# Last column of a mixture-of-experts tail: the last pair's combine ahead of the gate products, one gather pass and one gain row moved, overflow counts made earlier

## The chip, the core and the metric

The kernel runs on one core of a Trainium2 chip. The metric is the device time of one execution in microseconds (us). The core has five engines with an instruction queue each: TensorE (PE, matrix products), VectorE (DVE), ScalarE (ACT), GpSimd (POOL) and SyncE (SP, which here issues the DMA transfers of weights and output rows). Each engine works through its own queue in order and waits on semaphores of the others.

## The reference

One decoder layer on 512 tokens of width 1024: a mixer (windowed attention and an mLSTM), cross-attention into 256 memory tokens, and a mixture of 64 experts; each of the three is followed by a layer norm of `alpha*h + branch`. The change lies in the third part:

```
g_sel = argmax(h @ w_router_group + b)                 # 1 of 8 groups
top_val, top_idx = top_k(expert logits of that group, 2)
weights = p_group * softmax(top_val)                   # 2 experts for a token
for each expert e, for its tokens x:
    y = (silu(x @ w_gate[e]) * (x @ w_up[e])) @ w_down[e]
moe[token] += weight * y
out = layer_norm(alpha*h + moe, ln3_g, ln3_b)
```

w_gate and w_up are 1024x256 and w_down 256x1024 for each expert, float32: three times 1 MB, 192 MB for the 64 experts.

## The kernel before

**Columns.** The expert part starts at about 720 us of the profile. The 1024 assignments of tokens to experts are put into 21 columns of 128 slots; a column serves 4 experts with 32 slots, 2 with 64, or 1 with 128. Two columns make a pair, whose tokens are gathered together by products with one-hot matrices (`gather`, L1261 and L1262, px copied to XT by ACT and DVE in `to_XT`, L1184 and L1182). For a column, `hidden` makes 8 x 4 gate products and as many up products for four experts (L1204, 64 instructions each in the profile), Silu on ACT (L1209) and the multiply with the up products on DVE (L1210); then come two transposes, a copy, the down products (L1285), a split of the scaled result into a high and a low part (`split`, L255 on ACT, L256 on DVE), and for each pair `combine`: one-hot products in eight tiles of 512 columns through two PSUM buffers (L1430), each added into the stream h by DVE (L1431). An assignment that finds no slot goes to an overflow loop behind the columns; its expert list and count (`ovi`) are made on DVE and moved by one PE transpose (`poe`) while columns 0 to 2 run.

**Weights.** Ten slots of 1 MB in SBUF are a ring that SP fills in order of use (L167, L171). A load into a slot waits for the last product that read it. The down weights of the last column (L184) are loaded in 12 pieces: for four experts columns 0 to 511, then 512 to 767, then 768 to 1023.

**The last column (c = 20).** It is alone, and its rows are finished without a combine. Its gate products (u = 0 in `hidden`) are followed by a hook at (0, 7), `rows_meanwhile`, in PE's order ahead of the up products. The hook holds the combine of the last pair (columns 18 and 19, tiles `pc_last`), then three gather passes `slot_rows` (L1578), which bring the stream's rows of the last column's tokens into PSUM tiles `zf` (512, 256 and 256 columns, 4 products each). Beside them the final layer norm runs for four row tiles of 128 tokens, each 128x1024: `stats` (bn_stats, L1531), `rsqrt2` for two row tiles (`ve` on DVE, L1537, and a power on POOL, L97), `shift2` (`nb`, DVE, L1542), `norm_row` (ACT, L1564), `gain_row` (DVE, L1567), `bias_row` (L1570; rows 0 and 1 on POOL, rows 2 and 3 on DVE) and a store by SP (L1571). The out tiles of these rows lie in two slots of the weight ring. Behind the up products come Silu, multiply, transposes `ph_l` (L1621), the copy (L1623), the down products `pd_l` (L1631), split, the products that add them to `zf` (L1635), bn_stats (L1637), the last norm steps on DVE and an indirect store from POOL (L1645) that writes the rows of the last column's tokens.

**Order.** For DVE and ACT the order of this part is that of the code (a manual schedule is switched on at L1525); PE and SP follow the order of the code, too. PSUM tiles come from pools, and a tile waits for the readers of the tile that had its bank before.

Of the kernel before, what the change touches and what calls it, by code (L numbers as in the profile page):

```python
# [10 lines left out]
F32 = mybir.dt.float32  # L11
# [5 lines left out]
ALU = mybir.AluOpType  # L17
AX = mybir.AxisListType
PSUM = bass.MemoryType.PSUM

P = 128
# [10 lines left out]
NE = 64  # L32
# [29 lines left out]
def tile_layer(ctx, tc, x, mem, positions, w_in, attn_sinks, conv_w, conv_b, b_igate, b_fgate, ml_norm_g,  # L62
# [4 lines left out]
    V, A, G, T = nc.vector, nc.scalar, nc.gpsimd, nc.tensor  # L67
# [11 lines left out]
    def tap(name, ap):  # L79
        if taps is not None and name in taps:  # L80
            nc.sync.dma_start(taps[name], ap)
# [13 lines left out]
    def rsqrt_cols(dst, src, n):  # L95

        G.tensor_tensor(dst, src, pow_h.to_broadcast([P, n]) if n > 1 else pow_h, ALU.pow)  # L97

    class LayerNorm:
# [7 lines left out]
        def stats(self, c):  # L107
            V.bn_stats(self.st[:, c, :], self.r[:, c * 512:(c + 1) * 512])
# [107 lines left out]
    work = scope.enter_context(tc.tile_pool(name="work_a", bufs=2))  # L216
# [32 lines left out]
    def split(hi, lo, src, scale=None, on=V):  # L249

        if scale is None:
            A.copy(hi, src)
            on.tensor_tensor(lo, src, hi.bitcast(F32), ALU.subtract)
        else:
            A.activation(hi, src, AF.Copy, scale=scale)  # L255
            V.scalar_tensor_tensor(lo, src, scale, hi.bitcast(F32), op0=ALU.mult, op1=ALU.subtract)  # L256
# [57 lines left out]
    def run(gen):  # L314
        for _ in gen:
            pass
# [432 lines left out]
    work = scope.enter_context(tc.tile_pool(name="work_x", bufs=2, reuse_waits="tile"))  # L749
# [81 lines left out]
    work = scope.enter_context(tc.tile_pool(name="work_y", bufs=2, reuse_waits="tile"))  # L831
# [80 lines left out]
    work = Arena(poolY, "arenaR")  # L912
    scr_at = 0
    R = work.tile([P, 8, P], name="R")
    iota_f = keep.tile([P, S], F32, name="iota_f")
    G.iota(iota_f, pattern=[[1, S]], base=0, channel_multiplier=0, allow_small_or_imprecise_dtypes=True)
    iota_p = work.tile([P, 1], name="iota_p")
# [37 lines left out]
    scr64 = work.tile([P, 1, NE], F32, name="scr64")  # L955
# [299 lines left out]
    def gather(g, XT, tag, pool, n=256):  # L1255

        for c in range(4):
            px = pool[0].tile([P, 2, 256], F32, name=f"px{tag}{c}", tag=pool[1])
            for j in range(2):
                for t in range(NT):  # L1260
                    T.matmul(px[:, j, :n], lhsT=h2hv[:, t, 2 * c + j, :], rhs=g[:, t, :n], start=(t == 0), stop=False)  # L1261
                    T.matmul(px[:, j, :n], lhsT=h2lv[:, t, 2 * c + j, :], rhs=g[:, t, :n], start=False, stop=(t == NT - 1))  # L1262
            to_XT(XT, px, c, n)
            yield
# [24 lines left out]
    def pair_onehots(tag):  # L1289
        t = strm.tile([P, 1056], F32R, name=f"oh{tag}", tag="wr", bufs=4)  # L1290
        return [t[:, i * S:(i + 1) * S] for i in range(2)]

    def scaled(pds, tok, wcol, oh, tag):

        yh = strm.tile([P, 1056], F32R, name=f"yh{tag}", tag="wh", bufs=2)[:, :D]
        yl = strm.tile([P, 1056], F32R, name=f"yl{tag}", tag="wl", bufs=2)[:, :D]
        V.tensor_scalar(oh, iota_f, tok, None, op0=ALU.is_equal)
        for nh, pd in enumerate(pds):
            ns = slice(nh * 512, (nh + 1) * 512)
            split(yh[:, ns], yl[:, ns], pd, wcol)  # L1300
        return yh, yl, oh

    exc = key
    ovend = work.tile([P, NE], F32, name="ovend")
    ovst = work.tile([P, NE], F32, name="ovst")
# [47 lines left out]
    pds01 = [[next(down0)]]  # L1353
# [5 lines left out]
    pds01.append(list(down(first[1], parts_of(1), "1", (psA, "psA"))))  # L1359
    used[0] += COLS[0][0] + COLS[1][0]  # L1360
    wstream.ahead(used[0] + len(wslots))
    gi = work.tile([P, 2, NT * 2], I32, name="gi")
    cs_ = work.tile([P, 2, NT * 2], F32, name="cs_")
    gflat = gslot.rearrange("p t k -> p (t k)")
# [21 lines left out]
    wtab = keep.tile([P, NCOL], F32, name="wtab")  # L1386
    tokf = keep.tile([P, NCOL], F32, name="tokf")
    g1 = gather(G1, XTs[1], "1", (psB, "psB"))
# [2 lines left out]
        T.matmul(ptab[:, :2 * NCOL], lhsT=R[:, i, :], rhs=CV[:, i].rearrange("p a c -> p (a c)"), start=(i == 0), stop=(i == 7))  # L1391
    V.tensor_scalar(wtab, ptab[:, 0:NCOL], 1.0 / ALPHA, None, op0=ALU.mult)
    V.tensor_scalar(tokf, ptab[:, NCOL:2 * NCOL], BIGIDX, None, op0=ALU.add)
    oh01 = pair_onehots("0")
    ys01 = [scaled(pds01[0], tokf[:, 0:1], wtab[:, 0:1], oh01[0], "0")]

    inb = exc
    ovc = work.tile([P, 1], F32, name="ovc")
    V.scalar_tensor_tensor(inb, ovst, iota_p, iota_f[:, :NE], op0=ALU.is_le, op1=ALU.mult)
    V.tensor_scalar(ovst, ovend, iota_p, None, op0=ALU.is_gt)  # L1400
    V.tensor_tensor_reduce(scr64[:, 0], inb, ovst, 1.0, 0.0, op0=ALU.mult, op1=ALU.add, accum_out=ovc)
    run(g1)
    poe = psB.tile([P, 512], F32, name="poe", tag="psB")
    T.transpose(poe[:1, 0:P], ovc, ident)
    ovi = keep.tile([1, 33], I32, name="ovi")
    V.tensor_copy(ovi[:, 0:32], poe[:1, 0:32])
    V.tensor_copy(ovi[:, 32:33], ovend[0:1, NE - 1:NE])
    ys01.append(scaled(pds01[1], tokf[:, 1:2], wtab[:, 1:2], oh01[1], "1"))
    tap("ovi", ovi)

# [6 lines left out]
    pb = ctx.enter_context(ExitStack())  # L1417
# [4 lines left out]
    def combine(ys, tag, pool=(psC, "psC")):  # L1422

        mms = [(oh, y) for yh, yl, oh in ys for y in (yh, yl)]
        for t in range(NT):
            for nh in range(2):
                ns = slice(nh * 512, (nh + 1) * 512)
                pc = pool[0].tile([P, 512], F32, name=f"pc_{tag}{t}{nh}", tag=pool[1])
                for i, (oh, y) in enumerate(mms):
                    T.matmul(pc, lhsT=oh[:, t * P:(t + 1) * P], rhs=y[:, ns], start=(i == 0), stop=(i == len(mms) - 1))  # L1430
                V.tensor_tensor(acc[:, t, ns], acc[:, t, ns], pc, ALU.add)  # L1431
                yield
# [28 lines left out]
    ys, before = [], ys01  # L1461
    for c in range(2, NMAIN - 1):
# [33 lines left out]
        if c % 2:  # L1496
            before, ys = ys, []
# [24 lines left out]
    def half(nh):  # L1522
        return slice(nh * 512, (nh + 1) * 512)
# [11 lines left out]
    def rsqrt2(t):  # L1535

        V.tensor_scalar(ve3[:, t:t + 2], mv3[:, t:t + 2, 1], LN_EPS / ALPHA ** 2, None, op0=ALU.add)  # L1537
        rsqrt_cols(rs3[:, t:t + 2], ve3[:, t:t + 2], 2)

    def shift2(t):  # L1540

        V.scalar_tensor_tensor(nb3[:, t:t + 2], mv3[:, t:t + 2, 0], -1.0, rs3[:, t:t + 2], op0=ALU.mult, op1=ALU.mult)  # L1542
# [13 lines left out]
    def out_tiles():  # L1556
        for i in range(2):
            pool, tag = wslots[wstream.next % wstream.total]
            wstream.next += 1
            t = pool.tile([P, 2048], F32, name=f"out{i}", tag=tag)  # L1560
            outt.extend([t[:, 0:D], t[:, D:2 * D]])

    def norm_row(t):
        A.activation(outt[t], acc[:, t, :], AF.Identity, bias=nb3[:, t:t + 1], scale=rs3[:, t:t + 1])  # L1564

    def gain_row(t):
        V.tensor_tensor(outt[t], outt[t], g3, ALU.mult)  # L1567

    def bias_row(t, on):
        on.tensor_tensor(outt[t], outt[t], b3, ALU.add)  # L1570
        nc.sync.dma_start(out[t * P:(t + 1) * P, :], outt[t])  # L1571

    def slot_rows(i):

        o, w_ = LASTD[i]
        zf.append(psL.tile([P, 512], F32, name=f"zf{i}", tag="psL")[:, :w_])
        for t in range(NT):
            T.matmul(zf[i], lhsT=gsel[:, t, :], rhs=acc[:, t, o:o + w_], start=(t == 0), stop=False)  # L1578

    zf = []  # L1580

    def rows_meanwhile():
        nonlocal psL
        run(combine(before, "last"))
        pb.close()
        psL = ctx.enter_context(tc.tile_pool(name="psL", bufs=6, space=PSUM, reuse_waits="tile"))
        for t in range(NT):
            for nh in range(2):
                zs[t, nh] = acc[:, t, half(nh)]
        wstream.ahead(used[0] + COLS[c][0] + len(wslots))  # L1590
        out_tiles()
        for i in range(3):
            slot_rows(i)
        for t in range(2):
            for nh in range(2):
                stats(t, nh)
        rsqrt2(0)
        for nh in range(2):
            stats(2, nh)
        shift2(0)  # L1600
        norm_row(0)
        norm_row(1)
        for nh in range(2):
            stats(3, nh)
        rsqrt2(2)
        gain_row(0)
        shift2(2)
        norm_row(2)
        norm_row(3)
        bias_row(0, G)  # L1610
        gain_row(1)
        bias_row(1, G)
        gain_row(2)
        gain_row(3)
    psL = None
    hb = hidden_of(c, (psU, "psU"), {(0, 7): rows_meanwhile})
    yh = strm.tile([P, 1056], F32R, name="yh_l", tag="wh", bufs=2)[:, :D]
    yl = strm.tile([P, 1056], F32R, name="yl_l", tag="wl", bufs=2)[:, :D]
    ph = psH.tile([P, 512], F32, name="ph_l", tag="psH")[:, :2 * P].rearrange("p (k n) -> p k n", k=2)
    for k in range(2):  # L1620
        T.transpose(ph[:, k, :], hb[:, k, :], ident)  # L1621
    hT = hTs[c % 2]
    V.tensor_copy(hT, ph)  # L1623
    bias_row(2, V)
    bias_row(3, V)
# [23 lines left out]
    psL = (psL, "psL")  # L1649
# [77 lines left out]
```

## Time and profile before

| what | value |
|---|---|
| median of 3 runs | 1237.27 us (1236.13 to 1238.44) |
| the profiled execution | 1236.06 us |
| span of its profile | 1234.3 us |
| PE busy, DVE, ACT, POOL | 1149.0, 619.0, 373.3, 120.0 us |
| read from HBM | 264.72 MB |

The span is the time from the first to the last instruction in the profile; around it lie 1.76 us of the profiled execution. A row of a timeline gives the start, the duration, engine, line and operation, what it writes and reads, and in brackets the idle time of the engine just before it with what ended that. Where several like instructions follow each other, one row holds them all (x64). The end of a product in the profile is modelled, so neighbours on PE overlap a little.

### The profile page before, as it was taken

The numbers are of one execution on the slowest core, as the hardware profiler recorded it, in microseconds if no ns is written. First come the engines' busy times: TensorE is split into PE (matmuls) and PEld (weight loads), VectorE is DVE, ScalarE is ACT, GpSimd is POOL, SyncE is SP. The second block draws the span as 40 slices with busy tenths as digits, with TensorE's granted clock in tenths as the row PEclk, the third lists the DMA queues.
The fourth block names the chain that finished last, engine by engine and source line by source line (L and its number), as shares of the span: only waits on it lengthen the run. The fifth ranks groups of instructions, "written<-read, shape, count | busy, mean of one in ns | idle before, by whom it ended". The sixth has DMA issues, their size and how long they took to land. (4 is left out here: it accounts for less than half of the span.)

```text
span 1234.3 us, 18464 instructions
## 1 busy us (share of the span) xinstructions
PE 1149.0 (93%) x7205; PEld 843.0 (68%) x7205; DVE 619.0 (50%) x1420; ACT 373.3 (30%) x709; POOL 120.0 (10%) x114
## 2 busy tenths in 40 slices
PE   6999999999999999999999999899979898988984
PEld 6777777777787788878888886555736565644542
DVE  5668986533334543584455587824314333422346
ACT  4334355434434422254344261011101011101012
POOL 1320010000010100142001110000000000000002
PEclk9999999999999999999999999999989899989997
DMA  7221112122223233725405159999999999999992
GB/s 190 86 69 52 52 52 69 53 84 69 68 73 98 78 94 110 243 87 160 123 23 205 35 226 402 394 419 419 410 419 419 419 392 419 418 419 418 419 404 96
DMA packets 118946, 268.07 MB, mean 217 GB/s; under 512 B 18752, under 2 KB 79168, under 8 KB 94792
## 3 DMA queue, kind: packets, MB, share of 16 engines
q1 hardware_dynamic: 118416, 265.78, 57.5%
q8 instruction: 58, 0.95, 0.3%
q10 hardware_dynamic: 296, 1.06, 0.3%
q14 instruction: 32, 0.26, 0.1%
q0 software_dynamic: 144, 0.02, 0.0%
HBM read 264.72 MB, written 2.62 MB: 217 GB/s over the span
## 5 line engine op out<-in xcount | busy, mean ns | idle before, releaser
L239 ACT CAST wh<-wr 128x1024 fp32r<-128x1024 f32 (+1 forms) x106 | 111.1, 1050 | 258.1 <-issue 81.9
L240 DVE TENSOR_TENSOR wl<-wr,wh 128x1024 fp32r<-128x1024 f32 (+1 forms) x80 | 99.3, 1242 | 152.3 <-ACT wh L239 147.1
L1204 PE MATMUL pu<-wu,arenaL 128*32 128x256 f32 (+2 forms) x1024 | 99.9, 435 | 28.1 <-DMA wu<-in_w_up_dram 28.1
L240 POOL TENSOR_TENSOR wl<-wr,wh 128x1024 fp32r<-128x1024 f32 x26 | 64.7, 2488 | 444.1 <-ACT wh L239 407.2
L1204 PEld LDWEIGHTS pu<-wu,arenaL 128*32 128x32 f32 (+2 forms) x1024 | 53.2, 133 | 70.4 <-DMA wu<-in_w_up_dram 37.0
L1204 PE MATMUL pu<-wg,arenaL 128*32 128x256 f32 (+2 forms) x1024 | 83.9, 389 | 10.9 <-DMA wg<-in_w_gate_dram 9.6
L1210 DVE TENSOR_TENSOR arenaR<-arenaR,pu 128x256 f32<-128x256 f32 x21 | 13.0, 621 | 145.2 <-ACT arenaR L1209 145.2
L1261 PE MATMUL px<-G,h2h 128*128 128x256 f32 (+1 forms) x320 | 81.2, 293 | 0.0
L1285 PE MATMUL pd<-wd,arenaR 128*32 128x512 f32 (+2 forms) x480 | 78.5, 596 | 1.5 <-DMA wd<-in_w_down_dram 1.1
L1204 PEld LDWEIGHTS pu<-wg,arenaL 128*32 128x32 f32 (+2 forms) x1024 | 46.5, 120 | 47.7 <-DMA wg<-in_w_gate_dram 13.6
L1262 PE MATMUL px<-G,h2l 128*128 128x256 f32 (+1 forms) x320 | 77.7, 282 | 0.0
L1431 DVE TENSOR_TENSOR h<-h,pc 128x512 f32<-128x512 f32 x72 | 49.4, 687 | 46.3 <-PE pc L1430 46.3
L1261 PEld LDWEIGHTS px<-G,h2h 128*128 128x128 f32 x320 | 61.0, 191 | 7.3 <-issue 7.3
L1209 ACT ACTIVATE arenaR<-pu 128x256 f32<-128x256 f32 x21 | 8.1, 384 | 190.3 <-PE pu L1204 190.3
L255 ACT ACTIVATE yh<-pd,wtab 128x512 fp32r<-128x512 f32 x40 | 26.3, 685 | 124.3 <-PE pc L1430 97.4
L1430 PE MATMUL pc<-yh,oh 128*128 128x512 f32 x144 | 60.9, 423 | 1.9 <-DVE h L1431 1.8
L1262 PEld LDWEIGHTS px<-G,h2l 128*128 128x128 f32 x320 | 61.2, 191 | 0.1
L1430 PE MATMUL pc<-yl,oh 128*128 128x512 f32 x144 | 56.8, 394 | 0.0
L1285 PEld LDWEIGHTS pd<-wd,arenaR 128*32 128x32 f32 (+2 forms) x480 | 23.7, 118 | 41.9 <-issue 32.3
L1184 ACT ACTIVATE arenaL<-px,gbk 128x256 f32<-128x256 f32 (+1 forms) x44 | 24.2, 554 | 71.5 <-PE px L1262 70.2
L97 POOL TENSOR_TENSOR rs<-ve,pow_h 128x2 f32<-128x2 f32 x2 | 2.4, 1224 | 440.6 <-DVE ve L1537 440.6
L1430 PEld LDWEIGHTS pc<-yh,oh 128*128 128x128 f32 x144 | 27.0, 187 | 24.6 <-DVE h L1431 14.0
(467 smaller groups left out, 2665.8 us busy)
## 6 DMA issues: line engine op xcount, KB each, us to landing
wg<-in_w_gate_dram SPq DMA_DIRECT2D x64, 1024.0 KB, 14.5
wu<-in_w_up_dram SPq DMA_DIRECT2D x64, 1024.0 KB, 14.6
wd<-in_w_down_dram SPq DMA_DIRECT2D x60, 1024.0 KB, 13.6
wr<-in_w_in_dram SPq DMA_DIRECT2D x50, 512.0 KB, 3.6
wr<-in_w_xkv_dram SPq DMA_DIRECT2D x16, 512.0 KB, 4.3
wr<-in_w_att_branch_dram SPq DMA_DIRECT2D x8, 512.0 KB, 3.8
wr<-in_w_ml_branch_dram SPq DMA_DIRECT2D x8, 512.0 KB, 3.9
wr<-in_w_mix_out_dram SPq DMA_DIRECT2D x8, 512.0 KB, 4.1
```

What stands on the lines that cost most here:

```text
L239: A.copy(hi, raw)
L240: (G if i % 4 == 3 else V).tensor_tensor(lo, raw, hi.bitcast(F32), ALU.subtract)
L255: A.activation(hi, src, AF.Copy, scale=scale)
L1184: A.activation(XT[:, k, :n], px[:, j, :n], AF.Identity, scale=gbk[:, 0, k:k + 1], bias=gbk[:, 1, k:k + 1])
L1204: T.matmul(pu[sl, u * 256:(u + 1) * 256], lhsT=XT[:, k, o + sl.start:o + sl.stop], rhs=w[what][:, k, :], start=(k == 0), stop=(k == NK - 1))
L1209: A.activation(hs, pu[:, 0:256], AF.Silu)
L1210: V.tensor_tensor(hb.rearrange("s k p -> s p k"), hs.rearrange("s (p k) -> s p k", k=2), pu[:, 256:512].rearrange("s (p k) -> s p k", k=2) ...
L1261: T.matmul(px[:, j, :n], lhsT=h2hv[:, t, 2 * c + j, :], rhs=g[:, t, :n], start=(t == 0), stop=False)
L1262: T.matmul(px[:, j, :n], lhsT=h2lv[:, t, 2 * c + j, :], rhs=g[:, t, :n], start=False, stop=(t == NT - 1))
L1285: T.matmul(pd[sl, :], lhsT=hT[:, k, sl], rhs=w['d'][:, k, nh * 512:(nh + 1) * 512], start=(k == 0), stop=(k == 1))
L1430: T.matmul(pc, lhsT=oh[:, t * P:(t + 1) * P], rhs=y[:, ns], start=(i == 0), stop=(i == len(mms) - 1))
L1431: V.tensor_tensor(acc[:, t, ns], acc[:, t, ns], pc, ALU.add)
```

## The change

It has two parts. At columns 0 to 2, three DVE operations that count overflow move from behind column 0's split to ahead of the tables for the slots, and the transpose `poe` with its two casts moves from behind the second half of the gather of columns 2 and 3 to ahead of it. At the last column, the combine of the last pair moves out of the hook to ahead of the gate products; the hook keeps two of the three gather passes; the third goes behind the up products; `shift2(2)` moves ahead of the first gain row; and the fourth gain row moves behind the multiply, directly ahead of the copy of the transposes.

```diff
@@ -1359,6 +1359,12 @@
     pds01.append(list(down(first[1], parts_of(1), "1", (psA, "psA"))))
     used[0] += COLS[0][0] + COLS[1][0]
     wstream.ahead(used[0] + len(wslots))
+
+    inb = exc
+    ovc = work.tile([P, 1], F32, name="ovc")
+    V.scalar_tensor_tensor(inb, ovst, iota_p, iota_f[:, :NE], op0=ALU.is_le, op1=ALU.mult)
+    V.tensor_scalar(ovst, ovend, iota_p, None, op0=ALU.is_gt)
+    V.tensor_tensor_reduce(scr64[:, 0], inb, ovst, 1.0, 0.0, op0=ALU.mult, op1=ALU.add, accum_out=ovc)
     gi = work.tile([P, 2, NT * 2], I32, name="gi")
     cs_ = work.tile([P, 2, NT * 2], F32, name="cs_")
     gflat = gslot.rearrange("p t k -> p (t k)")
@@ -1391,20 +1397,14 @@
         T.matmul(ptab[:, :2 * NCOL], lhsT=R[:, i, :], rhs=CV[:, i].rearrange("p a c -> p (a c)"), start=(i == 0), stop=(i == 7))
     V.tensor_scalar(wtab, ptab[:, 0:NCOL], 1.0 / ALPHA, None, op0=ALU.mult)
     V.tensor_scalar(tokf, ptab[:, NCOL:2 * NCOL], BIGIDX, None, op0=ALU.add)
-    oh01 = pair_onehots("0")
-    ys01 = [scaled(pds01[0], tokf[:, 0:1], wtab[:, 0:1], oh01[0], "0")]
-
-    inb = exc
-    ovc = work.tile([P, 1], F32, name="ovc")
-    V.scalar_tensor_tensor(inb, ovst, iota_p, iota_f[:, :NE], op0=ALU.is_le, op1=ALU.mult)
-    V.tensor_scalar(ovst, ovend, iota_p, None, op0=ALU.is_gt)
-    V.tensor_tensor_reduce(scr64[:, 0], inb, ovst, 1.0, 0.0, op0=ALU.mult, op1=ALU.add, accum_out=ovc)
-    run(g1)
     poe = psB.tile([P, 512], F32, name="poe", tag="psB")
     T.transpose(poe[:1, 0:P], ovc, ident)
     ovi = keep.tile([1, 33], I32, name="ovi")
     V.tensor_copy(ovi[:, 0:32], poe[:1, 0:32])
     V.tensor_copy(ovi[:, 32:33], ovend[0:1, NE - 1:NE])
+    oh01 = pair_onehots("0")
+    ys01 = [scaled(pds01[0], tokf[:, 0:1], wtab[:, 0:1], oh01[0], "0")]
+    run(g1)
     ys01.append(scaled(pds01[1], tokf[:, 1:2], wtab[:, 1:2], oh01[1], "1"))
     tap("ovi", ovi)
 
@@ -1577,19 +1577,18 @@
         for t in range(NT):
             T.matmul(zf[i], lhsT=gsel[:, t, :], rhs=acc[:, t, o:o + w_], start=(t == 0), stop=False)
 
+    run(combine(before, "last"))
+    pb.close()
+    psL = ctx.enter_context(tc.tile_pool(name="psL", bufs=6, space=PSUM, reuse_waits="tile"))
     zf = []
 
     def rows_meanwhile():
-        nonlocal psL
-        run(combine(before, "last"))
-        pb.close()
-        psL = ctx.enter_context(tc.tile_pool(name="psL", bufs=6, space=PSUM, reuse_waits="tile"))
         for t in range(NT):
             for nh in range(2):
                 zs[t, nh] = acc[:, t, half(nh)]
         wstream.ahead(used[0] + COLS[c][0] + len(wslots))
         out_tiles()
-        for i in range(3):
+        for i in range(2):
             slot_rows(i)
         for t in range(2):
             for nh in range(2):
@@ -1603,23 +1602,23 @@
         for nh in range(2):
             stats(3, nh)
         rsqrt2(2)
+        shift2(2)
         gain_row(0)
-        shift2(2)
         norm_row(2)
         norm_row(3)
         bias_row(0, G)
         gain_row(1)
         bias_row(1, G)
         gain_row(2)
-        gain_row(3)
-    psL = None
     hb = hidden_of(c, (psU, "psU"), {(0, 7): rows_meanwhile})
     yh = strm.tile([P, 1056], F32R, name="yh_l", tag="wh", bufs=2)[:, :D]
     yl = strm.tile([P, 1056], F32R, name="yl_l", tag="wl", bufs=2)[:, :D]
+    slot_rows(2)
     ph = psH.tile([P, 512], F32, name="ph_l", tag="psH")[:, :2 * P].rearrange("p (k n) -> p k n", k=2)
     for k in range(2):
         T.transpose(ph[:, k, :], hb[:, k, :], ident)
     hT = hTs[c % 2]
+    gain_row(3)
     V.tensor_copy(hT, ph)
     bias_row(2, V)
     bias_row(3, V)
```

PE at the last column, before: from the end of the gate products (`pu` from `wg`) by the combine (`pc_last`) and the gather passes (`zf`) to the up products (`wu`) and the transposes.

```order
L1430 MATMUL pc_last_10266<-yl_9937,oh_9935 128x512
L1430 MATMUL pc_last_10266<-yh_10126,oh_9935 128x512
L1430 MATMUL pc_last_10266<-yl_10127,oh_9935 128x512
L1578 MATMUL zf_10296<-h_3991,arenaL 128x512 x4
L1578 MATMUL zf_10301<-h_3991,arenaL 128x256 x4
L1578 MATMUL zf_10306<-h_3991,arenaL 128x256 x4
L1204 MATMUL pu_10191<-wu_10066,arenaL 32x256
...
L1204 MATMUL pu_10191<-wu_10153,arenaL 32x256
L1621 MATMUL ph_l<-ident,arenaR 128x128 x2
```

The same place of the changed kernel, from the last gate products on; the combine stands ahead of their first.

```order
L1204 MATMUL pu_10245<-wg_10018,arenaL 32x256
L1204 MATMUL pu_10245<-wg_10030,arenaL 32x256
L1204 MATMUL pu_10245<-wg_10042,arenaL 32x256
L1204 MATMUL pu_10245<-wg_10054,arenaL 32x256
L1578 MATMUL zf_10296<-h_3991,arenaL 128x512 x4
L1578 MATMUL zf_10301<-h_3991,arenaL 128x256 x4
L1204 MATMUL pu_10245<-wu_10066,arenaL 32x256
...
L1204 MATMUL pu_10245<-wu_10153,arenaL 32x256
L1578 MATMUL zf_10371<-h_3991,arenaL 128x256 x4
L1619 MATMUL ph_l<-ident,arenaR 128x128 x2
```

Ahead of the gather passes now stand gate products and no longer the combine, and the third pass stands between the up products and the transposes.

DVE at the last column, a piece of the difference (- before, + changed): from the variances of rows 2 and 3 (`ve`) over the shift (`nb`), the gain rows (`out` from `g`) and the multiply (from `pu`) to the copy (from `ph_l`).

```order
 L1537 TENSOR_SCALAR ve_10157<-mv_10156 128x2
-L1567 TENSOR_TENSOR out_10294<-out_10294,g_10112 128x1024
 L1542 SCALAR_TENSOR_TENSOR nb_10159<-mv_10156,rs_10158 128x2
-L1567 TENSOR_TENSOR out_10294<-out_10294,g_10112 128x1024
-L1567 TENSOR_TENSOR out_10295<-out_10295,g_10112 128x1024 x2
-L1210 TENSOR_TENSOR arenaR<-arenaR,pu_10191 128x128x2
-L1623 COPY arenaR<-ph_l 128x256
+L1567 TENSOR_TENSOR out_10294<-out_10294,g_10112 128x1024 x2
+L1567 TENSOR_TENSOR out_10295<-out_10295,g_10112 128x1024
+L1210 TENSOR_TENSOR arenaR<-arenaR,pu_10245 128x128x2
+L1567 TENSOR_TENSOR out_10295<-out_10295,g_10112 128x1024
+L1622 COPY arenaR<-ph_l 128x256
```

The shift moved ahead of all gain rows, and one gain row moved from ahead of the multiply to between multiply and copy. On ACT and SP the order of the last column is as it was.

DVE between column 1 and the tables for the slots, in the changed kernel: the counts (L1365 to L1367), the first of the operations that build the tables (L1371), and further on the table's values (`wtab`, `tokf`), the casts and the one-hot rows of column 0.

```order
L1365 SCALAR_TENSOR_TENSOR arenaR<-arenaR,iota_f 128x64
L1366 TENSOR_SCALAR arenaR<-arenaR 128x64
L1367 ISA arenaR<-arenaR 128x64
L1367 ISA arenaR 128x1
L1371 CAST arenaR<-gslot 128x8
...
L1398 TENSOR_SCALAR wtab<-ptab 128x53
L1399 TENSOR_SCALAR tokf<-ptab 128x53
L1403 CAST ovi<-poe 1x32
L1404 CAST ovi<-arenaR 1x1
L1297 TENSOR_SCALAR oh_6535<-iota_f,tokf 128x512
```

Before, the counts and the casts stood behind the splits of column 0, the casts behind the last gather copies.

## Rows read from the trace of the kernel before

**Rows 1.** Windows: length, PE, PEld, DVE, ACT, POOL busy, clock, DMA share, GB/s

```profile
800.00:1180.00 380.00, 344.82 (x2837) 213.61 (x2840) 126.72 (x243) 48.75 (x87) 0.00 (x0) 0.96 1.01 416
```

**Rows 2.** Timeline of PE at the last column

```profile
1178.29 3.64 PE L1285 MATMUL pd<-wd,arenaR 128*32 128x512 f32 x32
...
1184.34 0.62 PE L1204 MATMUL pu<-wg,arenaL 128*32 128x256 f32 x2 [1.44 <-DMA wg<-in_w_gate_dram]
1186.85 3.64 PE L1204 MATMUL pu<-wg,arenaL 128*32 128x256 f32 x58 [1.88 <-DMA wg<-in_w_gate_dram]
1190.41 0.50 PE L1430 MATMUL pc_last<-yh,oh 128*128 128x512 f32 x1
...
1198.32 7.15 PE L1578 MATMUL zf<-h,arenaL 128*128 128x512 f32 x24
1205.40 3.66 PE L1204 MATMUL pu<-wu,arenaL 128*32 128x256 f32 x64
1215.87 0.69 PE L1621 MATMUL ph_l<-ident,arenaR 128*128 128x128 f32 x2 [6.80 <-DVE arenaR L1210]
1217.07 6.34 PE L1631 MATMUL pd_l<-wd,arenaR 128*32 128x512 f32 x48 [0.52 <-DVE arenaR L1623]
```

**Rows 3.** Timeline of DVE at the last column

```profile
1183.57 0.86 DVE L1520 TENSOR_SCALAR arenaL<-prow,arenaR 128x128 f32<-128x128 f32 x3
...
1198.52 0.69 DVE L1431 TENSOR_TENSOR h<-h,pc_last 128x512 f32<-128x512 f32 x1 [0.26 <-PE pc_last L1430]
...
1205.17 0.17 DVE L1537 TENSOR_SCALAR ve<-mv 128x2 f32<-128x2 f32 x1
...
1207.20 2.32 DVE L1542 SCALAR_TENSOR_TENSOR nb<-mv,rs 128x2 f32<-128x2 f32 x1 [0.59 <-POOL rs L97]
1209.44 1.21 DVE L1567 TENSOR_TENSOR out<-out,g 128x1024 f32<-128x1024 f32 x1
1210.88 4.42 DVE L1567 TENSOR_TENSOR out<-out,g 128x1024 f32<-128x1024 f32 x2 [0.22 <-ACT out L1564]
...
1216.59 0.42 DVE L1623 COPY arenaR<-ph_l 128x256 f32<-128x256 f32 x1 [0.78 <-PE ph_l L1621]
...
1224.40 1.42 DVE L1637 BATCH_NORM_STATS2 stf<-zf 128x6 f32<-128x256 f32 x4
```

**Rows 4.** Timeline of POOL at the last column

```profile
1202.33 0.71 POOL L97 TENSOR_TENSOR rs<-ve,pow_h 128x2 f32<-128x2 f32 x1 [438.22 <-DVE ve L1537]
1205.42 1.74 POOL L97 TENSOR_TENSOR rs<-ve,pow_h 128x2 f32<-128x2 f32 x1 [2.38 <-DVE ve L1537]
1207.14 2.37 POOL L1570 TENSOR_TENSOR out<-out,b 128x1024 f32<-128x1024 f32 x1
1210.74 2.34 POOL L1570 TENSOR_TENSOR out<-out,b 128x1024 f32<-128x1024 f32 x1 [1.23 <-DVE out L1567]
```

**Rows 5.** Timeline of ACT at the last column

```profile
1209.61 2.37 ACT L1564 ACTIVATE out<-h,nb,rs 128x1024 f32<-128x1024 f32 x2 [3.45 <-PE pu L1204]
```

**Rows 6.** Windows of 3 us, columns as in Rows 1

```profile
958.00:961.00 3.00, 0.89 (x6) 0.34 (x10) 0.00 (x0) 0.00 (x0) 0.00 (x0) 0.79 1.00 415
1183.00:1186.00 3.00, 0.62 (x2) 0.14 (x2) 1.43 (x4) 0.00 (x0) 0.00 (x0) 1.00 1.00 407
1210.00:1213.00 3.00, 0.00 (x0) 0.00 (x0) 2.78 (x2) 2.25 (x3) 2.26 (x1) 0.89 0.44 175
1213.00:1216.00 3.00, 0.14 (x1) 0.14 (x2) 2.81 (x3) 0.00 (x0) 0.08 (x1) 0.50 0.44 175
```

**Rows 7.** The down weights from 1165 us by tile: issue to landing

```profile
DMA to landing us min/median/max: 6.5/9.8/14.5
```

**Rows 8.** Timeline of PE and DVE ahead of column 2's gate products

```profile
766.74 0.28 DVE L1399 SCALAR_TENSOR_TENSOR arenaR<-arenaR,iota_f 128x64 f32<-128x64 f32 x1
...
768.89 0.54 DVE L1182 TENSOR_SCALAR arenaL<-px,gbk 128x256 f32<-128x256 f32 x1 [0.86 <-ACT arenaL L1184]
...
769.57 3.66 PE L1204 MATMUL pu<-wg,arenaL 128*32 128x256 f32 x64 [1.21 <-DVE ovi L1407]
```

## Prediction

> **What bounds the kernel now.** I read the windows first. From 800 to 1180 us the core waits for its expert weights: the DMA engines show a share of 1.01 and 416 GB/s throughout [rows 1]. The change adds, removes and resizes no load, so that stretch can only be shifted as a whole. What is left is the tail, and there I read the timelines of PE, DVE, POOL and ACT side by side. On PE [rows 2] the reader sees two waits for the last gate weights (1.44 and 1.88), then the combine of the last pair from 1190.41, the three gather passes from 1198.32, the up products from 1205.40 to 1209.06, and then 6.80 us in which PE has nothing to do: its transposes at 1215.87 wait for the multiply on DVE (the wait names its tile, L1210). DVE is late because of row work that the last column does not need [rows 3]: two gain rows from 1210.88 take 4.42, where a gain row alone takes 1.21 at 1209.44. The down products begin at 1217.07 and take 6.34 for what takes 3.64 at full clock earlier (1178.29) [rows 2]; the granted clock is 0.89 in 1210 to 1213 and 0.50 behind it [rows 6]. From the first bn_stats of the last rows at 1224.40 to the end of the span (1234.3) are 9.9 us of a serial chain, which the change does not touch.
>
> **Combine ahead of the gate products.** Before, PE idled 3.32 in the two waits while the combine was queued behind them in PE's order. Now the combine comes first. PE can begin before 1184.34 - 1.44 = 1182.9, but two PSUM buffers hold its output, and DVE takes its first add only when it is through with the one-hot rows, at 1183.57 + 0.86 = 1184.43 [rows 3]. So the third of eight output tiles can begin at 1184.43 + 0.69 (one add) = 1185.1. A tile took (1198.32 - 1190.41)/8 = 0.99 [rows 2], longer than an add, so six more end at 1191.05, and the last add starts 0.2 later as it did before (1198.52 against 1198.32): 1191.25, that is 7.3 earlier. Everything that hangs on the finished rows (statistics, norm, gain, bias, gather passes) moves by that.
>
> **Gate products, passes, up products.** 64 gate products take what the 64 up products take, 3.66 [rows 2]: 1194.7, with no wait, since the last gate weight was there at 1186.85. Two of the passes are 768 of 1024 columns, 0.75 x (1205.40 - 1198.32) = 5.3: 1200.0. Up products: 1203.7. Their weights: the gate weights landed at 1184.34 and 1186.85, 2.5 apart in a full queue, so four up weights are there by 1196.8; hidden by 3.2. The third pass (1.77) runs while ACT and DVE do Silu and multiply, and PE has its transposes done at about 1206.0.
>
> **The loads that the gate products release.** Behind the gate products in SP's queue stand the 12 pieces of the last down weights; from the third on they stand behind slots that the last gate products read, so these move from 1190.4 to 1194.7, 4.3 later. The queue does not run dry at once: up weights until 1196.8, and two pieces of half a weight (1.25 each) until 1199.3. A piece took at least 6.5 from issue to landing [rows 7]: 1201.2, where 1199.3 + 1.25 = 1200.6 would lose nothing. So the pieces come 0 to 0.7 us late (4.3 if nothing covered them). The first half is needed at 1209 and the last piece 2.7 later; four weights at 2.5 each behind 1196.8 land at 1206.8, so 0.7 costs nothing and even 4.3 fits. The output rows lie in slots of these gate weights too; the first norm row needs the last add (1191.25), the statistics and POOL's power before it, so the slots are free by then.
>
> **Rows on DVE, ACT and POOL.** The variances of rows 2 and 3 are ready for POOL at 1205.17 - 7.3 + 0.17 = 1198.05; POOL's power took 0.71 alone and 1.74 beside a gain row [rows 4]. The first gain row now stands behind the shift (nb) and not ahead of it, so 0.71 applies: with a shift as short as the 0.17 of its neighbour, 1199.0. The two last norm rows take 2.37 on ACT [rows 5]: 1201.4, so Silu no longer stands behind them when the up products end at 1203.7 (before, until 1209.61 + 2.37 = 1212.0). Then come four gain rows on DVE (1.21 each) and two bias rows on POOL (2.36 each). The trace shows that they do not overlap: the shift at 1207.20 ends at 1209.52, with the bias row that began at 1207.14 and ended at 1209.51, and the gain pair at 1210.88 lost 2.0 to the bias row at 1210.74 [rows 3, 4]. They can be served in several orders. Three gains and the first bias row fill 1199.0 to 1205.0; the second bias row, long waiting, takes its turn while DVE does the multiply, and holds the fourth gain row, which the change puts directly ahead of the copy L1623, until 1207.3. In all of the orders but one the copy comes behind all six: 1199.0 + 4 x 1.21 + 2 x 2.36 = 1208.6; plus the copy's 0.42, down products from **1209.05** instead of 1217.07: **8.0 earlier**. In the exception the second bias row slips in ahead of the third gain and the sum is 0.7 later.
>
> No row shows a multiply of which one input is in PSUM beside a bias row of POOL. If it were held too, it would end at 1207.9, with transposes and the fourth gain row behind it: 1209.65, 0.6 later. The Trainium skill, page "SBUF — State Buffer", section "Who interferes with whom", says that a DVE instruction contends with a GpSimd instruction that reads SBUF when both of its inputs come from SBUF, and not with one such input. By that page the multiply goes free and the gain row ahead of the copy does not; no run here shows the first, the rows above agree on the second.
>
> **Down products at full clock.** With the clock at 1.00 they take 3.64 instead of 6.34 [rows 2]: **2.7 more**. PE would stand idle from 1206.0 to 1209.05, 3.0 us; before, PE was idle from 1209.06 to 1215.87, and the clock fell within 1210 to 1213 (0.89) [rows 6]. The rows do not decide a wait of that size: with PE busy for 0.89 of 3 us the clock fell in 958 to 961 (0.79), and with 0.62 of 3 us it did not in 1183 to 1186 (1.00) [rows 6]. I take 1.00 and keep 2.7 for the range.
>
> **Column 2.** The gate products of column 2 wait 1.21 for the casts of the overflow counts [rows 8]. Now counts and casts are done before; but the PSUM bank that these products then take was read by the last gather copy on DVE, at 768.89 + 0.54 = 769.43, 0.1 before the products began. So the wait only gets another name. The transpose for the counts, now ahead of the second gather half, costs PE under 0.2 (two transposes of 128x128 took 0.69 at half clock [rows 2]); the three count operations, 0.28 or less each [rows 8], I take to be covered by DVE's slack ahead of the tables. Net 0; the bounds are -1.2 (the whole wait) and +0.8 (all three exposed). Whatever it is goes straight through the load-bound stretch behind it, because these products free the slots of the next loads.
>
> **Sum.** 8.0 + 2.7 + 0 = 10.7. The profiled execution took 1236.06 (span 1234.3 and 1.76 around it): 1225.4. It was 1.2 below the median of the runs, 1237.27; from that, **1226.6**.
>
> **Rivals.**
> 1. *The clock falls in the 3.0 us before the down products.* For it: 0.79 in 958 to 961. Against: 1.00 in 1183 to 1186. Price 2.7: 1229.3.
> 2. *Nothing holds the fourth gain row* (POOL's bias rows done before, or sharing). Then PE sets the copy: transposes at 1206.0, down products at about 1206.5, no idle time: 2.5 less, 1224.1. Against it: the rows of the gain pair.
> 3. *The wait for the multiply is only exchanged for one for the down weights*, the case on the other side. Their issues now stand behind the combine. The last piece is needed at 1211.8; every us behind that costs one. Nothing is gained if it lands at 1211.8 + 10.7 = 1222.5, 15.7 later than 1206.8, and the kernel is slower by 0.2% behind 1225. For it is only the shift of ten issues, 4.3; against it that the queue holds work until 1199.3.
> 4. *The change does not do what it says at the end*: the copy waits for rows just as before, since gain rows still come first on DVE. Then only the 7.3 of the earlier combine would be gained and the half clock stays: 1230.0. Rival 1 is near to it, and they share a chance.
>
> **Chances.** Forecast, with the clock at 1.00 and the fourth gain row held: 0.44, its own range 1225.4 to 1227.5 (column 2's bounds and the 0.7 of the orders). Rivals 1 and 4 together 0.32. Rival 2 0.14. Pieces late by a few us, with or without the clock: 0.04. Nothing gained, 0.03, or slower, 0.03. The range for 8 in 10 leaves out the last three and the outer edge of rivals 1 and 2 with column 2's bounds: 1223.8 to 1230.2. A measurement of this kernel tells about 0.2%, 2.5 us, from no change. Faster 0.94, same 0.03, slower 0.03.
>
> **What the profile of the changed kernel would show.** PE: combine begun before 1183 and ended near 1191, gate products with no wait for a weight, third pass directly behind the up products at about 1203.7. DVE: the last add near 1191.3, a fourth gain row far longer than 1.21 directly ahead of the copy, and the copy ending near 1209. PE idle ahead of the down products for about 3 us, their duration 3.6 (clock 1.00) or over 5 (rival 1). Down products waiting for a DMA would be rival 3. In front of column 2's gate products a wait of about 1.2 for a gather copy. The forecast is wrong if the copy ends before 1207 or after 1211, or if the stretch up to 1180 is longer by more than 1.

## Result and the profile after

The changed kernel took 1225.07 us in the median of 4 runs (1224.01 to 1226.77), the kernel before 1236.7 (4 runs, 1235.73 to 1238.44): ratio 0.9906, 95% interval 0.9889 to 0.9923, 11.6 us less. Forecast were 1226.6 and 10.7 less. The profiled execution took 1224.48, its span is 1222.8.

PE at the last column of the changed kernel, by its timeline, the rows that answer to [rows 2]:

```profile
1178.01 3.64 PE L1285 MATMUL pd<-wd,arenaR 128*32 128x512 f32 x32
...
1181.82 0.48 PE L1430 MATMUL pc_last<-yh,oh 128*128 128x512 f32 x1
...
1184.80 0.50 PE L1430 MATMUL pc_last<-yh,oh 128*128 128x512 f32 x1 [0.87 <-DVE h L1431]
...
1190.80 3.66 PE L1204 MATMUL pu<-wg,arenaL 128*32 128x256 f32 x64
1194.39 5.43 PE L1578 MATMUL zf<-h,arenaL 128*128 128x512 f32 x16
1199.74 3.66 PE L1204 MATMUL pu<-wu,arenaL 128*32 128x256 f32 x64
1203.34 1.99 PE L1578 MATMUL zf<-h,arenaL 128*128 128x256 f32 x8
1205.17 0.38 PE L1619 MATMUL ph_l<-ident,arenaR 128*128 128x128 f32 x2
1208.11 3.65 PE L1630 MATMUL pd_l<-wd,arenaR 128*32 128x512 f32 x48 [2.56 <-DVE arenaR L1622]
```

The gate products have no bracket: nothing waits for a weight there any more. The only idle time of PE behind them is 2.56 ahead of the down products, and it is ended by the copy on DVE, not by a load. The down products take 3.65.

DVE and POOL of the same kernel, by their timelines, answering to [rows 3, 4]:

```profile
1190.90 0.69 DVE L1431 TENSOR_TENSOR h<-h,pc_last 128x512 f32<-128x512 f32 x1 [0.25 <-PE pc_last L1430]
...
1198.54 0.16 DVE L1542 SCALAR_TENSOR_TENSOR nb<-mv,rs 128x2 f32<-128x2 f32 x1 [0.81 <-POOL rs L97]
1198.74 5.68 DVE L1567 TENSOR_TENSOR out<-out,g 128x1024 f32<-128x1024 f32 x3
1204.35 0.60 DVE L1210 TENSOR_TENSOR arenaR<-arenaR,pu 128x256 f32<-128x256 f32 x1
1204.79 2.92 DVE L1567 TENSOR_TENSOR out<-out,g 128x1024 f32<-128x1024 f32 x1
1207.64 0.41 DVE L1622 COPY arenaR<-ph_l 128x256 f32<-128x256 f32 x1
...
1212.73 1.41 DVE L1636 BATCH_NORM_STATS2 stf<-zf 128x6 f32<-128x256 f32 x4
```

```profile
1197.80 0.70 POOL L97 TENSOR_TENSOR rs<-ve,pow_h 128x2 f32<-128x2 f32 x1 [2.39 <-DVE ve L1537]
1200.05 6.59 POOL L1570 TENSOR_TENSOR out<-out,b 128x1024 f32<-128x1024 f32 x2 [1.54 <-DMA wd<-in_w_down_dram]
```

Three gain rows take 5.68 where three times 1.21 is 3.63, and the fourth takes 2.92, until POOL is through with its second bias row at 1200.05 + 6.59 = 1206.64 and one gain row more. The multiply in between takes its usual 0.60 while the same bias row runs: a bias row that nothing holds takes 2.36 [rows 4], so this one was at work from about 1204.3.

Executions differ ahead of the tail: the down products of the last pair (L1285), the last work that stands in the same place in all kernels, started between 1176.3 and 1180.9 us in the 13 profiles. So tails are compared from that start, S. The table is worked out from the profiles of this study (start of `pd_l` and end of the span, minus S); labels are those of the experiments below.

| kernel | S | pd_l starts at S + | pd_l takes | span ends at S + |
|---|---|---|---|---|
| before | 1178.29 | 38.78 | 6.34 | 56.0 |
| changed | 1178.01 | 30.10 | 3.65 | 44.8 |
| e1 columns 0 to 2 alone | 1179.34 | 39.23 | 4.79 | 55.1 |
| e2 last column alone | 1177.29 | 30.09 | 3.65 | 44.8 |
| e3 combine alone | 1177.14 | 31.22 | 5.24 | 47.5 |
| e4 all but the combine | 1176.95 | 40.63 | 6.02 | 57.5 |
| f1 without POOL's bias rows | 1177.11 | 28.07 | 3.65 | 42.8 |
| f2, g2 fourth gain row behind the copy | 1176.34, 1179.67 | 28.06, 28.07 | 3.65, 3.65 | 43.5, 42.9 |
| f3 two more rows ahead of the copy | 1180.29 | 32.37 | 6.15 | 49.5 |
| f4 third pass in the hook | 1180.92 | 30.10 | 3.65 | 44.5 |
| g1 changed, once more | 1177.17 | 30.08 | 5.34 | 46.3 |
| g3 bias row 2 on DVE behind the copy | 1177.18 | 28.05 | 3.65 | 43.5 |

Where nothing behind S waits for a load, the start of `pd_l` repeats to some hundredths of a us between executions of kernels with the same order. The three kernels that keep the combine in the hook (before, e1 and e4) hang on the last gate weight, too: its wait ended at S + 8.56 before, at S + 7.33 in e1 and at S + 8.99 in e4. The length of `pd_l` does not repeat, and that is the clock (below).

### The profile page after: what moved, and what is told of

Same layout as the page of the kernel before. It is cut to its first block, busy times and chain, and to the rows that moved or that the text cites. A ratio compares the mean times of both kernels' runs of the same rounds, so it can differ in the third digit from the quotient of the medians.

```text
span 1222.8 us, 18463 instructions
## 1 busy us (share of the span) xinstructions
PE 1143.1 (93%) x7205; PEld 842.2 (69%) x7205; DVE 618.1 (51%) x1420; ACT 373.5 (31%) x709; POOL 120.8 (10%) x114
## 5 line engine op out<-in xcount | busy, mean ns | idle before, releaser
L1204 PE MATMUL pu<-wu,arenaL 128*32 128x256 f32 (+2 forms) x1024 | 93.6, 415 | 26.0 <-DMA wu<-in_w_up_dram 26.0
L1285 PE MATMUL pd<-wd,arenaR 128*32 128x512 f32 (+2 forms) x480 | 80.1, 596 | 4.4 <-DMA wd<-in_w_down_dram 4.1
L1204 PEld LDWEIGHTS pu<-wg,arenaL 128*32 128x32 f32 (+2 forms) x1024 | 46.3, 121 | 45.6 <-issue 11.1
L1285 PEld LDWEIGHTS pd<-wd,arenaR 128*32 128x32 f32 (+2 forms) x480 | 23.0, 118 | 47.0 <-issue 33.3
## 6 DMA issues: line engine op xcount, KB each, us to landing
wg<-in_w_gate_dram SPq DMA_DIRECT2D x64, 1024.0 KB, 14.6
```

The costliest lines, as they stand in the source:

```text
L1204: T.matmul(pu[sl, u * 256:(u + 1) * 256], lhsT=XT[:, k, o + sl.start:o + sl.stop], rhs=w[what][:, k, :], start=(k == 0), stop=(k == NK - 1))
L1285: T.matmul(pd[sl, :], lhsT=hT[:, k, sl], rhs=w['d'][:, k, nh * 512:(nh + 1) * 512], start=(k == 0), stop=(k == 1))
```

## Experiments

**e1 and e2: the two parts apart.** e1 has the kernel before's last column, e2 its columns 0 to 2.

```diff
 e1, against the kernel before
...
+    V.scalar_tensor_tensor(inb, ovst, iota_p, iota_f[:, :NE], op0=ALU.is_le, op1=ALU.mult)
...
     gi = work.tile([P, 2, NT * 2], I32, name="gi")
...
+    T.transpose(poe[:1, 0:P], ovc, ident)
...
     oh01 = pair_onehots("0")
...
 e2, against the kernel before
+    run(combine(before, "last"))
...
-        for i in range(3):
+        for i in range(2):
...
+    slot_rows(2)
...
+    gain_row(3)
     V.tensor_copy(hT, ph)
```

> Only the part at columns 0 to 2 (counts, transpose and casts earlier). My theory: the wait ahead of column 2's gate products stays near 1.2 us and is only ended by the last gather copy instead of the casts; time within 1 us of the kernel before. Rival: some of the 11.6 us come from here; then 1 us or more faster than before.

> Only the part at the last column. My theory: all of the gain, 11 to 12 us faster than the kernel before, as the full change. Rival: the full change's gain holds a share of column 2, and this one gains 10.5 us or less.

e1: 1236.82 against 1236.81, ratio 1.0001 (0.9992 to 1.001). e2: 1223.98 against 1236.81, ratio 0.99 (0.9884 to 0.9917). So the part at columns 0 to 2 is worth nothing that the times show (the interval is about 1 us to either side), and the last column all. The wait ahead of column 2's gate products in e1's timeline of PE:

```profile
770.52 3.66 PE L1204 MATMUL pu<-wg,arenaL 128*32 128x256 f32 x64 [1.24 <-DVE arenaL L1182]
```

Its name changed from the cast (L1407 in [rows 8]) to the last gather copy, its length from 1.21 to 1.24.

**e3 and e4: the combine alone, and all but the combine.**

```diff
 e3: before, with
+    run(combine(before, "last"))
+    pb.close()
+    psL = ctx.enter_context(tc.tile_pool(name="psL", bufs=6, space=PSUM, reuse_waits="tile"))
     zf = []
     def rows_meanwhile():
-        nonlocal psL
-        run(combine(before, "last"))
...
 e4: the change, with these lines in the hook as before
```

> Only the combine of the last pair ahead of the gate products; three passes in the hook, shift and gain rows in the old order. My theory: the row chain on DVE and POOL sets the copy and hangs on the last add, so it moves by 7.3 us and the transposes behind it with it; down products near 1209.5. 7.5 us faster than before if the clock falls in the idle time of about 3.4 us ahead of the transposes, 10.3 if it does not. Rival: the parts share the gain, since passes and gain rows still stand ahead of Silu's multiply; then 5 us or less.

> The full change but for the combine, which stays in the hook; passes, shift and gain row as in the change. My theory: the last add stays at 1198.5, gain and bias rows still need some 9 us behind the shift at about 1206.1, and the clock still falls while PE waits: 1 to 2 us faster than before. Rival: PE's order (third pass behind the up products, gain row behind the multiply) frees the multiply and the transposes by itself: 4 us or more.

e3: 1226.81 against 1236.81, ratio 0.9921 (0.9907 to 0.9934), 10.0 us less. e4: 1236.57, ratio 0.9999 (0.999 to 1.0008). On the same chip e2, with all edits of the last column, gained 12.8, so the combine alone brings most of it (the intervals of the two overlap); its down products start 7.56 earlier from S (38.78 to 31.22). The rows of PE in e3:

```profile
1200.61 3.66 PE L1204 MATMUL pu<-wu,arenaL 128*32 128x256 f32 x64
1207.40 0.44 PE L1619 MATMUL ph_l<-ident,arenaR 128*128 128x128 f32 x2 [3.13 <-DVE arenaR L1210]
1208.36 5.24 PE L1629 MATMUL pd_l<-wd,arenaR 128*32 128x512 f32 x48 [0.52 <-DVE arenaR L1621]
```

Here PE idles 3.13 and 0.52, and the down products take 5.24, between the two lengths: the clock was down in part of them (0.70 in 1207 to 1210, 0.73 in 1210 to 1213, 1.00 behind that). e3's gain lies between the two that were named. e4 did not show the 1 to 2 us that I expected. Its profile says why it cannot be seen in the time of that execution: the two waits for gate weights are in front of the gate products again, and behind them the clock was down.

```profile
1183.45 0.62 PE L1204 MATMUL pu<-wg,arenaL 128*32 128x256 f32 x2 [1.87 <-DMA wg<-in_w_gate_dram]
1185.94 6.46 PE L1204 MATMUL pu<-wg,arenaL 128*32 128x256 f32 x58 [1.87 <-DMA wg<-in_w_gate_dram]
...
1214.48 0.44 PE L1621 MATMUL ph_l<-ident,arenaR 128*128 128x128 f32 x2 [3.31 <-DVE arenaR L1210]
1217.58 6.02 PE L1632 MATMUL pd_l<-wd,arenaR 128*32 128x512 f32 x48 [2.66 <-DVE arenaR L1624]
```

58 gate products took 6.46 instead of 3.64 in [rows 2], and the two waits are 0.42 longer together, so the last add started at S + 23.47 and not at S + 20.23 as before:

```profile
1200.42 0.69 DVE L1431 TENSOR_TENSOR h<-h,pc_last 128x512 f32<-128x512 f32 x1 [0.25 <-PE pc_last L1430]
```

From the last add to the start of `pd_l` are 17.16 us in e4 and 17.21 in the changed kernel, but 18.55 before, 18.54 in e1 and 18.32 in e3. So behind the last add the other edits shorten the chain by 1.1 to 1.4. This is worked out from one profile each. The times of e4, whose interval reaches from 1.2 less to 1.0 more, do not show it, and how often the clock falls in those waits was not measured.

**f1: the hold on DVE's rows.** POOL's bias rows 0 and 1 are left out, so these two row tiles are stored without the bias.

```diff
-        bias_row(0, G)
+        nc.sync.dma_start(out[0:P, :], outt[0])
...
-        bias_row(1, G)
+        nc.sync.dma_start(out[P:2 * P, :], outt[1])
```

> The full change with POOL's two bias rows (rows 0 and 1) left out, so these rows are stored without the bias. My theory (a bias row on POOL and a gain row on DVE do not overlap): the fourth gain row takes 1.2 instead of 2.9 us, the copy comes 1.9 us earlier, 13.5 us faster than the kernel before. Rival (the fourth gain row is slow for another reason, or PE sets the copy): as the full change, 11.6 faster.

1221.63 against 1236.74, ratio 0.9878 (0.9862 to 0.9895), 15.1 less. DVE in f1:

```profile
1197.85 3.50 DVE L1567 TENSOR_TENSOR out<-out,g 128x1024 f32<-128x1024 f32 x3
1203.09 0.62 DVE L1210 TENSOR_TENSOR arenaR<-arenaR,pu 128x256 f32<-128x256 f32 x1 [1.74 <-ACT arenaR L1209]
1203.54 1.21 DVE L1567 TENSOR_TENSOR out<-out,g 128x1024 f32<-128x1024 f32 x1
```

With no bias row on POOL, three gain rows take 3.50 and the fourth 1.21; the multiply takes 0.62, as it did beside the bias row. The down products start at S + 28.07, 2.03 earlier than in the changed kernel. That the two rows exclude each other, and that this reaches the down products, is shown.

**f2 and g2: the fourth gain row behind the copy.** Nothing is left out; all four bias rows run on POOL.

```diff
-    gain_row(3)
     V.tensor_copy(hT, ph)
-    bias_row(2, V)
-    bias_row(3, V)
+    gain_row(3)
+    bias_row(2, G)
+    bias_row(3, G)
```

> The full change with the fourth gain row behind the copy and all four bias rows on POOL. My theory: the copy follows the transposes at about 1205.6, down products near 1206.0 instead of 1208.1, about 2 us faster than the full change, 13.6 us faster than the kernel before. Rival: the last pieces of the down weights (which land near 1208.4) or POOL's longer list become the end, 12 us or less.

> The fourth gain row behind the copy, all bias rows on POOL, once more. My theory: its copy comes 2.0 us earlier, but the last row's store lands only after the last DVE operation, so 0.7 is given back; tail 43.5 us, 1.3 us faster than the full change. Rival: no difference to the full change that can be measured, as the earlier runs were on another chip.

f2: 1222.18 against 1236.74, ratio 0.9886 (0.9869 to 0.9902), 14.6 less. g2, on one chip with g1 and g3: 1223.96 against 1237.61, ratio 0.9889 (0.9873 to 0.9906), 13.7 less, with a tail of 42.9 where 43.5 was expected. The copy comes 2.0 earlier in both, the weights do not hold it, and bn_stats starts 2.04 earlier from S in f2; but the span ends only 1.3 (f2) and 1.9 (g2) earlier. What was given back shows in DVE's and POOL's rows of f2:

```profile
1212.28 1.41 DVE L1643 SCALAR_TENSOR_TENSOR arenaL<-arenaL,rsf,b 128x512 f32<-128x512 f32 x2
```

```profile
1198.37 12.24 POOL L1570 TENSOR_TENSOR out<-out,b 128x1024 f32<-128x1024 f32 x4 [1.54 <-DVE out L1567]
...
1215.24 1.21 POOL L1644 DMA_INDIRECT out_dram<-arenaL,tok_u  x1 [3.68 <-POOLq L1651]
```

DVE was through at 1213.69, the indirect store began 1.55 later; in the changed kernel it began 0.30 behind it (1217.70 behind 1217.40). POOL ended the last bias row at 1210.61, and the store of that row still had to go out (g3 below comes back to it).

**f3: a longer wait for the down products.**

```diff
+    bias_row(2, V)
+    bias_row(3, V)
     V.tensor_copy(hT, ph)
-    bias_row(2, V)
-    bias_row(3, V)
```

> The full change with the two bias rows of DVE ahead of the copy, so that PE is idle for 5 instead of 2.6 us ahead of the down products. My theory: the clock falls in that time, as it did in 6.8 us of the kernel before: 2.4 us for the rows and up to 2.7 for the down products, 6.5 to 7 us faster than the kernel before. Rival: the clock stays at 1.00; 9.2 faster.

1229.36 against 1236.74, ratio 0.9937 (0.9921 to 0.9954), 7.4 less. PE and the clock in f3:

```profile
1212.66 6.15 PE L1630 MATMUL pd_l<-wd,arenaR 128*32 128x512 f32 x48 [4.82 <-DVE arenaR L1624]
```

```profile
1207.00:1210.00 3.00, 0.83 (x5) 0.47 (x3) 3.00 (x3) 0.00 (x0) 1.92 (x1) 1.00 1.02 357
1210.00:1213.00 3.00, 0.34 (x4) 0.20 (x8) 2.60 (x3) 0.00 (x0) 0.00 (x0) 0.66 0.85 341
1213.00:1216.00 3.00, 3.00 (x16) 0.59 (x12) 0.00 (x0) 0.00 (x0) 0.00 (x0) 0.50 0.54 214
```

The clock was 1.00 until 1210, fell in the idle time and was 0.50 when the down products ran: 2.27 us for the two rows and 2.50 for the clock, 4.7 of tail against the changed kernel.

**f4: the third gather pass in the hook.**

```diff
-        for i in range(2):
+        for i in range(3):
             slot_rows(i)
...
-    slot_rows(2)
```

> The full change with the third gather pass back in the hook, ahead of the up products. My theory: the copy waits for the fourth gain row on DVE, not for PE, so up products, Silu and multiply 1.8 us later cost 0 to 0.3 us: 11.3 to 11.6 us faster than before. Rival: PE's order is on the path, 9.8 us faster.

1226.25 against 1236.74, ratio 0.9908 (0.9892 to 0.9925), 10.5 less. That lies between what was expected and the rival, and its interval holds both; the profile decides. `pd_l` starts at S + 30.10, to the hundredth where it started in the changed kernel; PE idles 1.24 and 1.30 instead of 2.56. The move of the third pass is worth nothing: DVE's rows set the copy.

**g1 and g3: the changed kernel again, and a further variant.** g3 tried to start the last row's store earlier.

```diff
-    gain_row(3)
     V.tensor_copy(hT, ph)
     bias_row(2, V)
-    bias_row(3, V)
+    gain_row(3)
+    bias_row(3, G)
```

> The full change once more, for a comparison with the next two on one chip. 11 to 12 us faster than the kernel before; tail from the down products of the last pair to the end of the span 44.8 us again.

> Behind the copy: bias row 2 on DVE, then the fourth gain row, then bias row 3 on POOL, so that POOL has one bias row less and the last store starts about 0.9 us earlier. My theory: the indirect store no longer waits for that store; tail 42.6 to 42.9 us, about 2 us faster than the full change. Rival: bias row and gain row on DVE hold the split of the down products, and the tail is 43.5 or longer.

g1: 1225.48 against 1237.61, ratio 0.9909 (0.9892 to 0.9925). g3: 1222.67, ratio 0.9891 (0.9874 to 0.9907). g1's tail was 46.3, not 44.8, and the reason is the clock alone, after the same wait:

```profile
1207.25 5.34 PE L1630 MATMUL pd_l<-wd,arenaR 128*32 128x512 f32 x48 [2.56 <-DVE arenaR L1622]
```

```profile
1204.00:1207.00 3.00, 0.70 (x5) 0.36 (x3) 3.00 (x3) 0.00 (x0) 1.78 (x1) 1.00 1.01 359
1207.00:1210.00 3.00, 2.75 (x20) 0.82 (x24) 2.46 (x3) 0.00 (x0) 0.00 (x0) 0.68 0.72 288
```

g3 did not do what I expected. Its bn_stats start at S + 32.68 as in f2, so the two rows on DVE hold nothing, which was the rival. The last row's store was issued 0.9 earlier from S than in f2, but it took 0.9 longer to land, as the tile of the out rows shows for that store in g3 and then in f2:

```profile
L1571 SPq DMA_DIRECT2D out_dram<-out x1: 333/333/333, 1210.6 to 1210.6; - x1
...
DMA to landing us min/median/max: 4.6/4.6/4.6
```

```profile
L1571 SPq DMA_DIRECT2D out_dram<-out x1: 332/332/332, 1210.6 to 1210.6; - x1
...
DMA to landing us min/median/max: 3.7/3.7/3.7
```

So it landed at S + 38.0 in both, and the indirect store began 0.9 to 1.0 behind that. In g2 the last store landed 3.1 after its issue at 1214.0, and the indirect store began 0.9 later, at 1218.04. That the indirect store waits for this landing fits all three, but it is not shown: in f1 it began 0.9 behind DVE's end (1215.38 behind 1214.46), though all stores had landed by 1212.6. Why the last store took longer in g3 stays open, too.

f2, g2 and g3 have medians 1.5 to 2.9 below those of the changed kernel (1225.07 and, as g1, 1225.48), but the intervals of their ratios overlap with its, and e2, whose last column is that of the change, had 1223.98; so by times they are not shown to beat it. Their tails, 42.9 to 43.5 against 44.8 to 46.3, say that they do by 1.3 or more.

## Why the prediction was right, step by step

**The last add.** Forecast 7.3 earlier; from S it moved from 20.23 (1198.52) to 12.89 (1190.90), 7.34. The wait on the add that I put ahead of the third tile is there, 0.87 at 1184.80. That this carries the tail is what e3 and e4 show: without the combine's move the times show no gain, with it alone 10.0.

**Gate products without waits.** As forecast. What I left out is that the clock can fall in these waits. In the two further kernels that have the combine in the hook, the 58 gate products behind the last wait took 5.33 (e1) and 6.46 (e4, above), against 3.64 in [rows 2]; the granted clock in 1186 to 1189 was 0.63 and 0.50:

```profile
1186.67 5.33 PE L1204 MATMUL pu<-wg,arenaL 128*32 128x256 f32 x58 [2.06 <-DMA wg<-in_w_gate_dram]
```

With the combine ahead of them no gate product waits, and in all ten profiles of such kernels the 64 took 3.66. How much this adds to the medians was not measured.

**The rows on DVE and POOL.** Forecast: shift ends at 1199.0, the copy behind four gain rows and two bias rows, down products at 1209.05. In the changed kernel, put on the S of before (0.28 later): shift ended at 1198.98, down products began at 1208.39. (The terms of that forecast add up to 1208.98, not 1209.05.) The mechanism is right, the term 4 x 1.21 + 2 x 2.36 = 9.56 was 0.6 too large: from 1198.74 to the end of the fourth gain row at 1207.71 are 8.97, since a row starts somewhat before the one ahead of it ends. In f1 three gain rows in a row take 3.50 and not 3.63, and in [rows 3, 4] the gain pair lost 2.0 to a bias row of 2.34. The early shift was forecast rightly, too: POOL's power took 0.70 and not the 1.74 that it took before beside this gain row of DVE:

```profile
1205.38 1.22 DVE L1567 TENSOR_TENSOR out<-out,g 128x1024 f32<-128x1024 f32 x1
```

**The multiply beside the bias row.** I had 0.6 in reserve if it were held. It took 0.60 at 1204.35 while the bias row ran, and 0.62 with none in f1: not held. The Trainium skill, page "SBUF — State Buffer", section "Who interferes with whom", lets a DVE instruction with one SBUF input pass beside a GpSimd instruction that reads SBUF and holds one with two. Here both were measured and agree: the multiply, and the fourth gain row (2.92 against 1.21).

**The clock.** I chose 1.00, for an idle time of 3.0 that the rows did not decide. It was 2.56. In the profiles with this wait the down products took 3.65 (changed, e2) and 5.34 (g1): both cases occur, so rival 1 is a part of the executions rather than another outcome, at 1.7 and not at its full price of 2.7. That the profiled execution had the 1.00 of the sum was luck: the rows did not decide it, and g1 shows the other case after the same wait. With 4.82 the clock fell (f3), with 0.52 alone it did not (f1, f2, g2, g3).

**Down weights.** Rival 3 fell: no wait for a load stands in front of `pd_l` in any profile, even where it starts 2 us earlier.

**Column 2.** Net 0, the wait renamed: as forecast, and e1 measures it at 1.0001.

**The sum.** From the profiled execution before I forecast 1225.4; the one after took 1224.48, 0.9 less. Of this, 0.66 is the earlier start of the down products from S (the rows above), and 0.28 is that S itself came earlier, which says nothing of the change; behind the down products 0.15 was lost. The gate products do not enter, as they ran at full clock in both of these executions. The median, 1225.07, is inside the range, but 0.3 below the forecast's own of 1225.4 to 1227.5. The upper end of that one does not follow from its two terms, 0.8 and 0.7, which give 1228.1.

**Rivals 2 and 4.** Rival 2, that nothing holds the fourth gain row, is refuted by 2.92 against f1's 1.21; its price, 2.5, was 2.03. Rival 4 is close to e3, the combine alone: rows still come first. It gained 10.0 and not 7.3; the down products took 5.24 in its profile and not the 6.34 of the half clock. e2 gained 12.8 on the same chip.

## What to carry to other kernels

When an engine idles for a load with independent work queued behind the wait, look at what hangs on that work. Here the two waits were 3.3 us of idle time on PE, but moving the combine ahead of them and of the gate products brought its last add forward by 7.3, and the row work of two other engines, nine us of it, starts behind that add. Measure a tail from the last event that is the same in both kernels; here the start of `pd_l` repeats to hundredths from there when no load is waited for in between, while whole executions differ by more than most of the single edits change. Moving an operation (third pass, counts) is worth nothing when something else ends the same wait, and f4 and e1 are the cheap way to find out.
